# Latent attention: the second rope product of the logits as a 128-row matmul with zero-padded low halves, and narrower raw weight buffers

## The chip, the cores and the metric

The kernel runs on one core of one Trainium2 chip, as one launch. The metric is the device time of that launch in microseconds (us). Engines are named as in the profile: PE is TensorE (PEld its weight loads), DVE is VectorE, ACT is ScalarE, POOL is GpSimd, SP issues the transfers.

## The reference, cut to what matters

The whole program is a stack of layers on 256 tokens of 1024 features, batch 1, all in float32: stick-breaking attention, a gated feed-forward layer with a convolution, forgetting attention, a second feed-forward layer, a pooling layer, and at the end latent attention (MLA) and a final norm. Only latent attention changes. It has 16 heads. A head's query and key have a part of 128 features of its own and a rope part of 64 features; the key's rope part is one for all heads:

```python
q = (rmsnorm_2(q_lat, q_norm_g) @ w_q_b).reshape(B, S, N_HEADS, QK_HEAD_DIM)   # 128 + 64
q_nope, q_rope = q[..., :QK_NOPE_DIM], q[..., QK_NOPE_DIM:]
...
q_rope = apply_rope(q_rope, cos[:, :, None, :], sin[:, :, None, :])
k_rope = apply_rope(k_rope, cos, sin)
...
s = (jnp.einsum('bqhd,bkhd->bhqk', qn, k_nope)
     + jnp.einsum('bqhr,bkr->bhqk', qr, k_rope)).astype(jnp.float32) * scale
s = jnp.where(mask, s, jnp.finfo(jnp.float32).min)
p = jax.nn.softmax(s, axis=-1).astype(v.dtype)
```

## The kernel before, in words

**Numbers in two halves.** Every float32 operand of a matmul is split into a high half and a low half, both of type float32r, and a product is made of three matmuls into one PSUM tile: high by high, high by low, low by high (`mm3`, lines 69 to 72). The high half is a copy on ACT (`hi_copy`, L55), the low half a subtraction on DVE (`lo_sub`, L59). So weights also pass through ACT and DVE before PE can use them.

**Weight streaming.** The weights come in chunks, in the order in which they are used; a chunk comes with one transfer on SP's queue into one of three raw buffers (`RAWB = 3`), each `RAWW` columns of float32 wide. ACT and DVE turn a chunk into parts of at most 1024 columns (tiles `wh`, `wl`, eight buffers each). `bg()` (L182) does this one part at a time and is called at fixed places between PE's work. When the last part of chunk c has been subtracted, `bg_lo` (L173 to L180) asks for chunk c + 3, whose transfer takes the raw buffer that has just come free. So what is counted ahead is chunks, whatever their size.

**Latent attention.** After the latents and their norms (`lat_norm`), `lat_T` (L1092) transposes them: queries' latents to `qT`, keys' to `kT`, and the key's rope part, which stands twice (in rows 0 to 63 and in rows 64 to 127), to `rT`; each with a high and a low tile. The heads are worked on in four groups g of four. For each group there are three chunks or more: two of 256 columns x 8 for the gate z (`m_z`), one of 3 x 768 columns for the queries (`m_q`, 2304 columns in all), one of 2 x 1024 for keys and values (`m_kv`), and in groups 1 to 3 the output projection's rows of the groups before (`m_o`), two chunks a group.

PE's order in the loop over g is written out by hand: `values(g)`, `logits(g, 0)`, `logits(g, 1)` (two heads each), the output projection of group g - 1 or the gate of the next group, `p_T` (transposes of the probabilities), `pv` (probabilities by values), then `q_rope`, `qk` and `rope_T` of the next group. Every engine takes its instructions in program order.

**The logits** (`logits`, L1158) of a pair of heads are made in two blocks: 128 keys for the first 128 queries, then 256 keys for the other 128. In a block each head has three 128-row matmuls for its own features (L70 to L72), then for the rope part one matmul of 128 rows at L1168 and one of 64 rows at L1170. `rope_T` has put a head's high halves in 64 rows of a tile `rq` and its low halves in the other 64 rows, so that the 128-row matmul against `rT`'s high tile does high by high and low by high at once. The 64-row matmul, high by low, reads only the high rows of `rq` and the same rows of `rT`'s low tile. For the pair's first head these are rows 0 to 63, for the second rows 64 to 127.

Of the kernel before, what the change touches and what calls it, by code (L numbers as in the profile page):

```python
# [7 lines left out]
F32 = mybir.dt.float32  # L8
F32R = mybir.dt.float32r
# [6 lines left out]
P = 128  # L16
S = 256
NT = S // P
D = 1024
# [7 lines left out]
RAWW = 2304  # L27
# [8 lines left out]
def tile_net(ctx: ExitStack, tc: tile.TileContext, t, out):  # L36
# [16 lines left out]
    # ---------------------------------------------------------------- helpers  # L53
# [10 lines left out]
    def split(hi, lo, src, scale=None):  # L64
        """src = hi + lo exactly, both of float32r's width"""
        hi_copy(hi, src, 1.0 if scale is None else scale)
        lo_sub(lo, src, hi, scale)
# [6 lines left out]
    def mm3s(ps, ls, rs, first, last):  # L74
        """sum over ls, rs; the low halves of ls last"""
        n = len(ls)
        for m in range(n):
            pe.matmul(ps, lhsT=ls[m][0], rhs=rs[m][0], start=first and m == 0, stop=False)  # L78
            pe.matmul(ps, lhsT=ls[m][0], rhs=rs[m][1], start=False, stop=False)
        for m in range(n):  # L80
            pe.matmul(ps, lhsT=ls[m][1], rhs=rs[m][0], start=False, stop=last and m == n - 1)
# [13 lines left out]
    def at(x, k, c):  # L95
        """columns c of k-tile k, high and low; x a pair of tiles or a list of such pairs,
        each of as many k-tiles"""
# [11 lines left out]
    # ------------------------------------------------------- weight streaming  # L109
    # A chunk [P, a, b] comes in with one transfer and is split in parts of at  # L110
    # most TW columns: by its first dimension ("k") or by columns ("c").  A part
    # is in use until `need` of its columns have gone into TensorE's program.
# [28 lines left out]
    def load_w(upto):  # L141
        while nxt["load"] <= min(upto, len(specs) - 1):
# [3 lines left out]
            # the first ones a part at a time  # L146
# [10 lines left out]
    def bg_hi():  # L157
        """the next part's high half, if there is room for it"""
# [30 lines left out]
    def get_w(i):  # L189
        """function (k, c0, n) -> the split columns of chunk i"""  # L190
# [16 lines left out]
    # ---- the order in which the weights are used  # L207
    def add_v(w, c0):
        """two halves of columns, each in two chunks of four k-tiles"""
# [11 lines left out]
    # the order of the down projection's sum  # L221
# [55 lines left out]
    for g in range(4):  # L277
        add_mz(g)
        wq = t["mla_w_q_b_2"][0][:, 768 * g:768 * (g + 1)]
        W["m_q", g] = rows(wq, 0, 3, need=4 * P + NT * 768)  # L280
# [5 lines left out]
    def get_rows(idx, n=2):  # L286
        """chunks of n k-tiles each -> function (k, c0, n)"""
# [3 lines left out]
    # -------------------------------------------------------------- residual  # L291
# [20 lines left out]
    # ------------------------------------------------------------- constants  # L312
# [7 lines left out]
    # [cos, cos] and [-sin, sin]  # L320
# [3 lines left out]
    # ------------------------------------------------------------------ norms  # L324
    def mean_sq(srcs, n):
        """mean of the squares of the rows of srcs, together n wide, + EPS: summands"""
# [14 lines left out]
    def transpose_split(src, dst, i, b, m=4):  # L341
        """src's column tiles b..b+m -> dst (hi, lo), token tile i"""
# [12 lines left out]
    def scaled(i, r, g):  # L355
        """h's token tile i, by its factor and the gain"""
# [6 lines left out]
    def norm_r(i):  # L363
        """the factor of the norm of h's token tile i"""
# [4 lines left out]
    def square(x, n, ss):  # L369
        """ss = sum of the squares of the rows of x over n"""  # L370
# [4 lines left out]
    # a layer's end: by halves of columns, then the rest  # L375
    def post_add(i, acc, g):
        """h += rmsnorm(acc) * g for token tile i"""
# [28 lines left out]
    # ------------------------------------------------------------ projections  # L406
    def proj_A(ps, aT, w, c0, nk, m=P):
        """ps [m features, S tokens]"""
# [3 lines left out]
    def out_rows(acc, i, oT, w, ks, first, last, by_half=False):  # L412
        """acc [token tile i, D] += o^T rows @ w rows; ks: (k of o^T, k of w)"""
# [8 lines left out]
    def nat_start(aT, views, hook):  # L422
        """two chunks of 256 columns, a token tile at a time; natural in SBUF"""
# [17 lines left out]
    def values_all(xT, views, vv, hooks):  # L441
        """vv = x W, by halves of columns and token tiles; hooks: (half, tile, k) -> what
        comes before the k-th step"""
# [18 lines left out]
    def nat_T(ps, xs, c):  # L462
        """column tile c of nat_start's result, transposed: ps [P, S]"""
# [3 lines left out]
    def edge(tail0, tail1, acc, add, g, dst):  # L467
        """end of a layer: token tile 0 ahead of 1, up to the next layer's
        input; returns that of tile 1, not yet transposed, and the factors"""
# [18 lines left out]
    def attention(s0, s1, s2, s3, post, w_ids, oT, g_post, dst, hook, late, acc0_tile):  # L488
        """the eight pairs of heads, a stage of each a step, in TensorE's
        order; then the output projection up to the next layer's input"""  # L490
# [36 lines left out]
    def heads_out(p, vv, pr, oT):  # L527
        """out^T of the pair's heads into oT"""
# [12 lines left out]
    # per-feature parameters, a feature a partition  # L541
# [22 lines left out]
    # ------------------------------------------------- stick-breaking layer  # L564
# [14 lines left out]
    with tc.tile_pool(name="sb", bufs=2) as sb, tc.tile_pool(name="sbv", bufs=1) as sbv:  # L579
# [6 lines left out]
        # constants of the layer  # L586
# [5 lines left out]
        # -1 where the row (a later key) is at or after the column  # L592
# [22 lines left out]
        def s1(p):  # L615
            qh, ql = st.pop(("qk", p))
            zt = [acc_tile("z") for j in range(2)]
            # z^T, columns (s0: t 0..255, s1: t 128..255), both heads
# [11 lines left out]
            # softplus(z) = max(z, 0) + ln(1 + e^-|z|)  # L630
# [12 lines left out]
        def s2(p):  # L643
            zt, nh, nl, _ = st.pop(("z", p))
            # z - sum of the softplus of the keys from s to t: the logarithm of A
# [35 lines left out]
    # --------------------------------------------------------------- conv FFN  # L681
    # the last steps of the down projection, one token tile after the other
    TAIL = (4, 5)

    def ffn(l, aT, a1, late, dst):
        """a1: token tile 1 of aT, not yet transposed; returns what edge() does;
        late: the gains after and of the next layer's input"""
# [60 lines left out]
    # --------------------------------------------------------- softmax pieces  # L748
    def causal_mask(m):
        """[t of a tile, s of the tile before and the tile itself]"""  # L750
# [4 lines left out]
    def softmax(pl_, zts, cmask, scale, bias=None, bufs=1, ahead=1):  # L755
        """zts: logits of two heads, (t0: 128 keys, t1: 256 keys); the probabilities in SBUF"""
# [29 lines left out]
    def prob_T(pt):  # L786
        """p^T of a head in [s, t] blocks: s0 x (t0, t1), s1 x t1"""
# [5 lines left out]
    with tc.tile_pool(name="fxa", bufs=1) as fxa:  # L793
# [5 lines left out]
        # ------------------------------------------------------ forgetting layer  # L799
        table_set(NLE_SET)  # L800
        with tc.tile_pool(name="fx", bufs=2) as fx, tc.tile_pool(name="fxv", bufs=1) as fxv:
# [17 lines left out]
            # causal mask of a query tile's own keys and those before  # L819
# [5 lines left out]
            # selectors: -1 in row h of each quarter  # L825
# [8 lines left out]
            # forget gates: cumulative log f, [head, t]  # L834
# [70 lines left out]
    # -------------------------------------------------------------- pool layer  # L905
    with tc.tile_pool(name="pl", bufs=2) as pl_, tc.tile_pool(name="plc", bufs=1) as plc:
        # 1 / count of the first 15 positions
# [119 lines left out]
        # MLA's latents: (columns from, columns, weights)  # L1027
# [16 lines left out]
    # --------------------------------------------------------------- MLA layer  # L1044
    with tc.tile_pool(name="ml", bufs=2) as ml, tc.tile_pool(name="mlc", bufs=1) as mlc:
        # the gains of both latents and the mask
# [7 lines left out]
        rT = [mlc.tile([P, 1, S], F32R, name=n) for n in ("rTh", "rTl")]  # L1054

        def rope(dst, src, m, i0, i1, nh):
            """dst, src: [P, token tiles i0..i1, nh, 64]; dst and m, for a product, in SBUF"""
# [34 lines left out]
        def lat_T(i):  # L1092
            transpose_split(lats[i], qT, i, 0, 3)
            transpose_split(lats[i], kT, i, 3, 2)
            transpose_split(lats[i], rT, i, 5, 1)
# [19 lines left out]
        def q_rope(g):  # L1115
            """q's rope part of four heads, natural"""
            wq = st["wq", g] = get_w(W["m_q", g])
# [23 lines left out]
        def rope_T(g):  # L1141
            qr = st.pop(("qr", g))
            pst = mm_tile("pst")
            # of a head: high halves in its own 64 rows, low halves in the others
# [13 lines left out]
        def logits(g, a):  # L1158
            rq = st["rq", g]
            zt = [acc_tile("z") for j in range(2)]  # L1160
            for c0, n, t0 in ((0, P, 0), (P, S, P)):
# [4 lines left out]
                for j in range(2):  # L1166
                    r = slice(64 * j, 64 * j + 64)
                    pe.matmul(zt[j][:, c0:c0 + n], lhsT=rq[j][:, a, t0:t0 + P],  # L1168
                              rhs=rT[0][:, 0, 0:n], start=False, stop=False)
# [272 lines left out]
```

## Time and profile before

| what | value |
|---|---|
| median of 3 runs | 1006.05 us |
| lowest and highest run | 1001.23 and 1006.25 us |
| the profiled execution, span from first to last instruction | 1007.2 us (the page gives no other time for it) |
| PE busy | 992.5 us, 99% of the span |
| DVE, ACT, POOL busy | 754.7, 607.8, 71.6 us |
| mean granted TensorE clock | 0.992 |

A busy PE is not PE at its peak: matmuls overlap, and the profile models their ends. The distance from one matmul's start to the next one's says more than its duration. The clock is given as a share of its upper level: 1.00 is 2.4 GHz, 0.50 is 1.2 GHz. Latent attention takes the last 200 us or so of the span.

### The profile page before, as it was taken

Reading aid. Unit: us, or ns where it says so; the run is one execution under the profiler, and the core shown is the slowest. Engines: PE = TensorE matmul, PEld = TensorE weight load, DVE = VectorE, ACT = ScalarE, POOL = GpSimd, SP = SyncE. Lnnn points to the kernel's source line nnn. Section 1 sums busy time; section 2 is a strip of 40 time slices with the busy share of each in tenths; the row PEclk is TensorE's granted clock in tenths of the full one; section 3 lists DMA queues with packets and bytes.
Section 4 is the critical chain, followed back from the end, with each engine's and each line's share of the span. In section 5 each row is a group of like instructions: output and inputs, shape, how many; then the busy total and the mean of one; then the engine's idle time right before and its main releaser. Section 6 shows DMA issues by size and latency. Waiting matters only on the chain.

```text
span 1007.2 us, 17578 instructions
## 1 busy us (share of the span) xinstructions
PE 992.5 (99%) x6955; PEld 909.0 (90%) x6955; DVE 754.7 (75%) x1297; ACT 607.8 (60%) x1050; POOL 71.6 (7%) x180
## 2 busy tenths in 40 slices
PE   8999999999999999999999999999999999999997
PEld 6899789999887899889999988999998899888986
DVE  5577788899745879877999944777677766967675
ACT  5489867677534657566667633664543546746563
POOL 1022220000002000020000000200000110110100
PEclk8999999999999999999999999999999999999999
DMA  8823346575752744426565664466554453534411
GB/s 292 258 86 145 126 163 214 167 244 177 251 183 79 239 134 168 142 84 209 185 224 179 202 240 143 153 224 230 170 167 146 145 186 123 172 127 138 159 66 42
DMA packets 116228, 170.79 MB, mean 170 GB/s; under 512 B 4162, under 2 KB 93618, under 8 KB 116146
## 3 DMA queue, kind: packets, MB, share of 16 engines
q1 hardware_dynamic: 116082, 169.68, 50.6%
q8 instruction: 54, 0.88, 0.4%
q14 instruction: 28, 0.23, 0.1%
q0 software_dynamic: 64, 0.00, 0.0%
HBM read 168.62 MB, written 1.05 MB: 168 GB/s over the span
## 4 chain that ended last, share of the span: by engine, by line
PE 93%; DVE 2%; ACT 2%; POOL 1%; DMA 1%; issue 1%; SPq 0%; POOLq 0%; DVEq 0%; ACTq 0%
PE psu L70 10%; PE psu L72 10%; PE psu L71 10%; PE accD L71 4%; PE accD L72 4%; PE accD L70 4%; PE psq L70 4%; PE psq L72 4%; PE psq L71 4%; PE accO L70 3%; PE accO L72 3%; PE accO L71 3%; PE accP L72 1%; PE accP L70 1%; PE accP L71 1%; PE accV L78 1%
## 5 line engine op out<-in xcount | busy, mean ns | idle before, releaser
L59 DVE TENSOR_TENSOR wl<-raw,wh 128x1024 fp32r<-128x1024 f32 (+3 forms) x300 | 353.0, 1197 | 105.9 <-ACT wh L55 103.1
L55 ACT ACTIVATE wh<-raw 128x1024 fp32r<-128x1024 f32 (+3 forms) x316 | 315.3, 1026 | 99.1 <-PE accD L72 44.2
L70 PE MATMUL psu<-aT,wh 128*128 128x256 f32 x864 | 241.7, 280 | 0.0
L72 PE MATMUL psu<-aT,wl 128*128 128x256 f32 x864 | 240.9, 279 | 0.0
L71 PE MATMUL psu<-aT,wh 128*128 128x256 f32 x864 | 240.8, 279 | 0.0
L72 PEld LDWEIGHTS psu<-aT,wl 128*128 128x128 f32 x864 | 162.3, 188 | 0.0
L70 PEld LDWEIGHTS psu<-aT,wh 128*128 128x128 f32 x864 | 162.1, 188 | 0.2
L71 PEld LDWEIGHTS psu<-aT,wh 128*128 128x128 f32 x864 | 162.0, 187 | 0.0
L703 DVE SCALAR_TENSOR_TENSOR yc<-psu,conv,yc 128x255 f32<-128x255 f32 (+1 forms) x160 | 73.4, 479 | 7.6 <-ACT yc L696 4.6
L70 PE MATMUL accD<-wh,gh 128*128 128x512 f32 x176 | 69.3, 394 | 0.0
L71 PE MATMUL accD<-wl,gh 128*128 128x512 f32 x176 | 69.3, 394 | 0.0
L72 PE MATMUL accD<-wh,gl 128*128 128x512 f32 x176 | 69.3, 394 | 0.0
L335 POOL TENSOR_TENSOR ss<-ss,epsc 128x1 f32<-128x1 f32 x24 | 10.9, 453 | 628.2 <-ACT junk L372 628.1
L70 PE MATMUL psq<-aT,wh 128*128 128x256 f32 x192 | 54.1, 282 | 0.1
L71 PE MATMUL psq<-aT,wh 128*128 128x256 f32 x192 | 53.5, 279 | 0.0
L72 PE MATMUL psq<-aT,wl 128*128 128x256 f32 x192 | 53.5, 278 | 0.0
L708 ACT ACTIVATE yc<-yc 128x256 f32<-128x256 f32 x44 | 18.4, 418 | 55.0 <-DVE yc L703 55.0
L696 ACT ACTIVATE yc<-psu,conv 128x256 f32<-128x256 f32 x80 | 40.3, 554 | 7.6 <-PE psu L72 7.6
L71 PEld LDWEIGHTS accD<-wl,gh 128*128 128x128 f32 x176 | 32.9, 187 | 8.1
L72 PEld LDWEIGHTS accD<-wh,gl 128*128 128x128 f32 x176 | 32.9, 187 | 8.1
L70 PEld LDWEIGHTS accD<-wh,gh 128*128 128x128 f32 x176 | 32.9, 187 | 8.1
L55 ACT ACTIVATE qkh<-psq 128x512 fp32r<-128x512 f32 x32 | 19.0, 594 | 33.0 <-PE psq L72 32.8
(331 smaller groups left out, 2288.9 us busy)
## 6 DMA issues: line engine op xcount, KB each, us to landing
raw<-in_w_up_dram SPq DMA_DIRECT2D x44, 1024.0 KB, 5.1
raw<-in_w_down_dram SPq DMA_DIRECT2D x22, 1024.0 KB, 5.0
raw<-in_pool_w_in_dram SPq DMA_DIRECT2D x16, 1024.0 KB, 7.1
raw<-in_sb_w_qkv_dram SPq DMA_DIRECT2D x10, 1024.0 KB, 6.1
raw<-in_w_kvf_dram SPq DMA_DIRECT2D x8, 1024.0 KB, 5.7
raw<-in_pool_w_out_dram SPq DMA_DIRECT2D x8, 1024.0 KB, 5.9
raw<-in_mla_w_in_dram SPq DMA_DIRECT2D x8, 1024.0 KB, 5.4
raw<-in_mla_w_out_dram SPq DMA_DIRECT2D x8, 1024.0 KB, 5.5
```

Source lines behind the costliest of these rows:

```text
L55: act.activation(out=hi, in_=src, func=AF.Copy, scale=scale)
L59: (eng or dve).tensor_tensor(out=lo, in0=src, in1=hi.bitcast(F32), op=ALU.subtract)
L70: pe.matmul(ps, lhsT=l[0], rhs=r[0], start=first, stop=False)
L71: pe.matmul(ps, lhsT=l[0], rhs=r[1], start=False, stop=False)
L72: pe.matmul(ps, lhsT=l[1], rhs=r[0], start=False, stop=last)
L78: pe.matmul(ps, lhsT=ls[m][0], rhs=rs[m][0], start=first and m == 0, stop=False)
L335: pool.tensor_tensor(out=s0, in0=s0, in1=epsc[:, 0:1], op=ALU.add)
L696: act.activation(out=y[:, u, :], in_=ps[:, u * S:(u + 1) * S], func=AF.Identity, bias=cp[:, 132 + q:133 + q], scale=cp[:, 88 + q:89 + q])
L703: dve.scalar_tensor_tensor(out=y[:, u, d:S], in0=ps[:, u * S:(u + 1) * S - d], scalar=w, in1=y[:, u, d:S], op0=ALU.mult, op1=ALU.add)
L708: act.activation(out=y[:, 0, :], in_=y[:, 0, :], func=AF.Gelu_apprx_tanh)
```

## The change

The key's rope part gets one high tile as before (`rTh`) and two low tiles, one for each head of a pair. `rTl[0]` has the low halves in rows 0 to 63 and zeros in rows 64 to 127, `rTl[1]` the other way round. The zeros are written once by POOL. The second rope matmul takes all 128 rows of `rq` and of the head's own low tile; the rows of low halves in `rq` meet zeros. `lat_T` does the rope part by itself, with one DVE subtraction for each of the two low tiles. The raw buffers shrink from 2304 to 2048 columns, which the query chunk does not fit; it becomes two chunks of 2 x 768 and 1 x 768 columns, read through `get_rows` instead of `get_w`. The parts and their order stay the same. The rest of the diff takes comments and docstrings out and moves line numbers.

```diff
-RAWW = 2304
+RAWW = 2048
...
-        W["m_q", g] = rows(wq, 0, 3, need=4 * P + NT * 768)
+        W["m_q", g] = [rows(wq, 2 * c, 2 - c, need=4 * P + NT * 768) for c in range(2)]
...
-        rT = [mlc.tile([P, 1, S], F32R, name=n) for n in ("rTh", "rTl")]
+        rTh = mlc.tile([P, S], F32R, name="rTh")
+        rTl = [mlc.tile([P, S], F32R, name=f"rTl{j}") for j in range(2)]
+        for j in range(2):
+            pool.memset(rTl[j].bitcast(F32), 0.0)
...
-            transpose_split(lats[i], rT, i, 5, 1)
+            ps = mm_tile("psT")
+            pe.transpose(ps[:, 0:P], lats[i][:, tok(5)], ident)
+            hi_copy(rTh[:, tok(i)], ps[:, 0:P])
+            for j in range(2):
+                r = slice(64 * j, 64 * j + 64)
+                lo_sub(rTl[j][r, tok(i)], ps[r, 0:P], rTh[r, tok(i)])
...
-            wq = st["wq", g] = get_w(W["m_q", g])
+            wq = st["wq", g] = get_rows(W["m_q", g])
...
                 for j in range(2):
-                    r = slice(64 * j, 64 * j + 64)
-                    pe.matmul(zt[j][:, c0:c0 + n], lhsT=rq[j][:, a, t0:t0 + P],
-                              rhs=rT[0][:, 0, 0:n], start=False, stop=False)
-                    pe.matmul(zt[j][:, c0:c0 + n], lhsT=rq[j][r, a, t0:t0 + P],
-                              rhs=rT[1][r, 0, 0:n], start=False, stop=True)
+                    for x in (rTh, rTl[j]):
+                        pe.matmul(zt[j][:, c0:c0 + n], lhsT=rq[j][:, a, t0:t0 + P], rhs=x[:, 0:n],
+                                  start=False, stop=x is not rTh)
```

On PE, the four rope matmuls of one block of the logits (first pair of heads, 128 keys; `rq` with its number is one head's tile):

```order
-L1168 MATMUL z<-rTh,rq_9525 128x128
-L1170 MATMUL z<-rTl,rq_9525 128x128
-L1168 MATMUL z<-rTh,rq_9526 128x128
-L1170 MATMUL z<-rTl,rq_9526 128x128
+L1178 MATMUL z<-rTh,rq_9532 128x128
+L1178 MATMUL z<-rTl_9078,rq_9532 128x128
+L1178 MATMUL z<-rTh,rq_9533 128x128
+L1178 MATMUL z<-rTl_9079,rq_9533 128x128
```

Their number and place stay; the second and the fourth now read a low tile of their own, over all rows.

On SP's queue, the weight transfers of latent attention from the first query chunk to the second group's (`mla_w_in` is the gate z, `mla_w_q_b` the queries, `mla_w_kv_b` keys and values, `mla_w_out` the output projection):

```order
-L153 DMA raw<-in_mla_w_q_b_dram 128x3x768
+L153 DMA raw<-in_mla_w_q_b_dram 128x2x768
+L153 DMA raw<-in_mla_w_q_b_dram 128x768
 L153 DMA raw<-in_mla_w_kv_b_dram 128x2x1024
 L153 DMA raw<-in_mla_w_in_dram 128x8x256 x2
-L153 DMA raw<-in_mla_w_q_b_dram 128x3x768
+L153 DMA raw<-in_mla_w_q_b_dram 128x2x768
+L153 DMA raw<-in_mla_w_q_b_dram 128x768
 L153 DMA raw<-in_mla_w_kv_b_dram 128x2x1024
 L153 DMA raw<-in_mla_w_out_dram 128x2x1024 x2
```

The order of the data is the same, but each query chunk takes two places. With three buffers, `m_kv` now waits for the buffer of the second chunk of z instead of the first, and the first chunk of `m_o` for the buffer of the query chunk's first piece instead of z's second chunk.

On DVE, the end of `lat_T` for one tile of 128 tokens (`psT` is the transposed latent, `wl` a weight part's low half):

```order
 L59 TENSOR_TENSOR kTl<-psT,kTh 128x2x128
-L59 TENSOR_TENSOR rTl<-psT,rTh 128x128
+L59 TENSOR_TENSOR rTl_9078<-psT,rTh 64x128
+L59 TENSOR_TENSOR rTl_9079<-psT,rTh 64x128
 L59 TENSOR_TENSOR wl<-raw,wh 128x768
```

One subtraction over 128 rows becomes two over 64 rows, ahead of the query weights' first part.

## Rows read from the trace of the kernel before

**Rows 1.** The page's head and its part 1, PE (busy us, share, instructions).
```profile
span 1007.2 us, 17578 instructions
PE 992.5 (99%) x6955; PEld 909.0 (90%) x6955; DVE 754.7 (75%) x1297; ACT 607.8 (60%) x1050; POOL 71.6 (7%) x180
```

**Rows 2.** The page's part 4, shares of the chain that ended last.
```profile
PE 93%; DVE 2%; ACT 2%; POOL 1%; DMA 1%; issue 1%; SPq 0%; POOLq 0%; DVEq 0%; ACTq 0%
```

**Rows 3.** Timeline of PE, first logits of group 0: start, duration (us), instruction, count.
```profile
837.85 0.27 PE L1168 MATMUL z<-rTh,rq 128*128 128x128 f32 x1
838.05 0.32 PE L1170 MATMUL z<-rTl,rq 64*128 64x128 f32 x1
...
838.81 0.39 PE L70 MATMUL z<-qkh 128*128 128x256 f32 x1
839.04 0.28 PE L71 MATMUL z<-qkl,qkh 128*128 128x256 f32 x1
...
839.64 0.28 PE L1168 MATMUL z<-rTh,rq 128*128 128x256 f32 x1
839.85 0.38 PE L1170 MATMUL z<-rTl,rq 64*128 64x256 f32 x1
...
840.78 0.33 PE L70 MATMUL z<-qkh 128*128 128x128 f32 x1
840.95 0.27 PE L71 MATMUL z<-qkl,qkh 128*128 128x128 f32 x1
```

**Rows 4.** Timeline of PE, logits of the forgetting layer, all of 64 rows.
```profile
361.56 0.28 PE L878 MATMUL z<-qkh,qkl 64*128 64x256 f32 x2
361.68 0.28 PE L883 MATMUL z<-F,sel 64*128 64x256 f32 x2
361.88 0.38 PE L70 MATMUL psq<-fTh,wh 128*128 128x256 f32 x1
```

**Rows 5.** Timelines of DVE and PE, first probabilities of group 0.
```profile
849.31 1.02 DVE L59 TENSOR_TENSOR pl<-pT,ph 128x384 fp32r<-128x384 f32 x2
...
853.48 0.28 PE L70 MATMUL po<-ph,vh 128*128 128x256 f32 x1
```

**Rows 6.** Timelines of SP, DVE and ACT, the weights behind group 0's logits.
```profile
848.10 11.53 SPq L153 DMA_DIRECT2D raw<-in_mla_w_out_dram  x2
...
857.41 4.10 DVE L59 TENSOR_TENSOR wl<-raw,wh 128x768 fp32r<-128x768 f32 x4
...
862.53 1.05 ACT L55 ACTIVATE wh<-raw 128x1024 fp32r<-128x1024 f32 x1
...
863.61 1.29 DVE L59 TENSOR_TENSOR wl<-raw,wh 128x1024 fp32r<-128x1024 f32 x1 [1.44 <-ACT wh L55]
```

**Rows 7.** DMA issues from 780 us on: count, KB each, us to landing.
```profile
raw<-in_mla_w_out_dram SPq DMA_DIRECT2D x8, 1024.0 KB, 5.5
```

**Rows 8.** Timeline of PE, the first values matmul of group 1.
```profile
869.34 0.50 PE L70 MATMUL psv<-wh,kTh 128*128 128x512 f32 x1 [0.17 <-DVE qkl L59]
```

**Rows 9.** Timelines of SP and DVE around the first query and key weights.
```profile
817.24 5.06 SPq L153 DMA_DIRECT2D raw<-in_mla_w_in_dram  x2
...
817.93 0.28 DVE L59 TENSOR_TENSOR rTl<-psT,rTh 128x128 fp32r<-128x128 f32 x1
...
824.97 3.45 DVE L59 TENSOR_TENSOR wl<-raw,wh 128x1024 fp32r<-128x1024 f32 x2
```

**Rows 10.** Timeline of PE, second logits up to the transposes, groups 1 and 2.
```profile
878.28 0.36 PE L70 MATMUL z<-qkh 128*128 128x256 f32 x1
...
888.45 0.82 PE L790 MATMUL pT<-ident,pt 128*128 128x128 f32 x6
...
926.98 0.28 PE L70 MATMUL z<-qkh 128*128 128x256 f32 x1
...
934.18 0.82 PE L790 MATMUL pT<-ident,pt 128*128 128x128 f32 x6
```

**Rows 11.** Windows; last columns are granted clock, DMA share, GB/s.
```profile
880.00:882.00 2.00, 2.00 (x5) 1.36 (x6) 1.97 (x9) 0.75 (x4) 0.00 (x0) 0.50 0.35 88
```

## The prediction

> **What bounds the kernel now.** I read the page first: PE is busy for 99% of a span of 1007.2 us [rows 1], and PE makes up 93% of the chain that ended last, while DVE, ACT and POOL have 2%, 2% and 1% of it [rows 2]. So a microsecond that PE gains is a microsecond gained, as long as no other engine is late at the place. Busy time doesn't tell whether PE is at its pace, so I read the timeline of PE in the logits next, from start to start [rows 3]. Among the matmuls of 128 rows a step is 0.12 us: five of them from 839.04 to 839.64. From the first rope matmul on the steps grow: 837.85 to 838.05 is 0.20, and the four rope matmuls with the matmul behind them take 837.85 to 839.04. The same rows with 256 keys show 839.64 to 840.95. The reader is to see that the long steps begin and end with the matmuls of 64 rows, and that the matmul after the last of them is slow too.
>
> Is a matmul of 64 rows slow by itself, or the change between 64 and 128 rows? In the forgetting layer's logits all have 64 rows [rows 4]. There a pair takes one step of 0.12 us, 361.56 to 361.68, so 0.06 each; the step from the last pair to the first 128-row matmul is 0.20. So the change of height costs, not the half height.
>
> **The rope matmuls, 32 of them in 16 blocks.** Their number stays. The block of 128 keys has five steps from the first rope matmul to the second one behind the block: 839.04 - 837.85 = 1.19 us. Five ordinary steps are 0.60, which saves 0.59. The block of 256 keys has 840.95 - 839.64 = 1.31, which saves 0.71. A call of `logits` has both, 1.30 us; eight calls give 10.4 us. The bounds: nothing saved if something other than the height sets these steps; and if the steps came down to the 0.06 of the forgetting layer's pairs, five would be 0.30, a call would save 1.90 and the eight 15.2. That end is out of reach, since those pairs work in different rows, and a padded matmul has no rows left for a neighbour. I take 10.4, because all matmuls in these blocks then have the form of those that make the 0.12 steps.
>
> Here a rule speaks against the change. The trace of the rope blocks shows no 64-row matmul beside another one [rows 3]. The Trainium skill, TensorE: Matmul & The Clock Gate (Part 3, packing small matmuls), says that matmuls of few rows run at the same time when they stand in different row groups, so that padding them to 128 rows would give a gain away. By that rule the 32 padded matmuls would lose 0.06 each, 1.9 us; by the row nothing is lost, since a 128-row matmul stands between any two of them. It is a rival below.
>
> **Does the gain reach the end?** In group 0 the two calls bring PE 2.6 us forward, while DVE, which works without a pause there, is not faster. PE's first product of probabilities and values at 853.48 would come at 850.88; DVE is through with the probabilities' low halves at 849.31 + 1.02 = 850.33 [rows 5]. That leaves 0.5 us, the tightest place. In groups 1 to 3 the output projection stands between, and there is more room. So DVE nearly becomes the bound, but doesn't.
>
> **The weights, which come later by one chunk.** The query chunk becomes two, so with three buffers each transfer behind it waits for a buffer one chunk younger. The first chunk of `m_o` started at 848.10, with great reserve. Now it waits until DVE has subtracted the query chunk's second part. That is the first of four parts that begin at 857.41 and take 4.10 us together [rows 6]; by columns it has 768 of 3584, 0.88 us, and ends at 858.3. A transfer of this size lands 5.5 us later [rows 7], at 863.8. ACT began to convert it at 862.53, DVE stood idle for 1.44 us until that was done [rows 6]. So conversion begins 1.3 us late. Behind it on ACT and DVE stand the rope products of the next queries and the splits of the next queries and keys, and for one of these PE already waits 0.17 us to get a PSUM buffer at 869.34 [rows 8]. All of the 1.3 us therefore reaches PE. If the whole stretch moves 2.6 us forward, so does each of these times. Bounds: 0, if the reserve of DVE is larger than these rows let see, and 5.5, a whole landing. I take 1.3, once.
>
> The first `m_kv` chunk gets the place in time of the transfer that started at 817.24 [rows 9]. It lands at 822.7 and takes ACT two conversions of 1.05 us each [rows 6], until 824.8; DVE takes it up at 824.97 [rows 9]. ACT's wait is covered by 0.2 us; without that cover each further microsecond of landing costs one. In groups 1 to 3 there are two chunks of `m_o` and two of the gate between, and the loads are due long after they land. Four more transfers on SP, which mostly waits, cost nothing.
>
> **DVE and POOL.** Two more subtractions of 0.28 us [rows 9], before the query weights' first part: 0 to 0.56, depending on whether PE waits for these parts. I take 0.3. The two clearings on POOL come when the tile's former users are long done; POOL's mean instruction is 71.6/180 = 0.4 us [rows 1], so 0.8 at most, and with 1% of the chain I take 0.
>
> **The clock.** In the second logits of group 1 the granted clock is at its lower level, 1.2 GHz (0.50) [rows 11]. From 878.28 to 888.45 the stretch takes 10.17 us, the same instructions in group 2 take 7.20, from 926.98 to 934.18 [rows 10]: 3.0 us. What PE did before: it waited for DVE [rows 8] and then went through the slow steps of the logits. The change removes the slow steps and lengthens the wait by 1.3 us. Groups 0, 2 and 3 have the slow steps too, but not the waits, and no fall of the clock. So the fall may go or stay. The three runs lie at 1006.05, 1001.23 and 1006.25; one without the fall would be 3.0 lower, which fits the lowest in sign, though not in all its size. I take it as gone, at little better than even odds.
>
> **The sum.** -10.4 + 1.3 + 0.3 = -8.8 us at an unchanged clock. The profiled execution goes from 1007.2 to 998.4; the median of the runs is 1.15 below its span, so 997.2. Without the fall of the clock, 994.2, which I round to 994.
>
> **The rivals.**
> - The fall of the clock stays: 997.2. For it: the longer wait ahead of the place. Against: the denser logits.
> - DVE or ACT becomes the bound in the loop: for it, DVE is at work without a pause from the logits to the probabilities, and the reserve in group 0 is 0.5 us. If each group gives back half of its 2.6 us, the gain shrinks by 5.2 and the time is 1002.4 with the fall of the clock and 999.4 without.
> - The change doesn't do what it says: the steps stay as they are, and the weights still come late: 1006.05 + 1.6 = 1007.7. If padding also lost the 0.06 us a matmul that the pairs of [rows 4] gain by running in different rows, 1.9 more: 1009.6. (That is the Trainium skill's rule of row groups, named above.) Against both, the 0.20 at the change of height in [rows 4] and the lone 64-row matmuls in [rows 3].
> - Slower: the late loads hit every group. The first `m_o` chunk shows the mechanism. Were each group to wait for a whole landing and one conversion, 5.5 + 1.05, the four lose 26 us against 10.4 gained: about 1022. It decides from 2.6 us a group on. Against it: only group 0 calls for its weights so closely behind each other.
> - More than forecast: the wait for `m_o` is absorbed, and the start too is like that of the lowest run: 1001.23 - 10.1, about 991.
>
> **How the numbers follow.** Forecast 50%, clock stays 30%, DVE bound 10%, no gain 4%, slower 3%, more 3%. Some 0.5% is what a measurement of this kernel can tell from no change, 5 us, so the border of faster is 1001.0. Forecast, staying clock, the last case and half of the DVE case lie beyond it: 0.88. The other half of the DVE case and the case of no gain make 0.09 for no difference, the late loads 0.03. The range reaches from 990, just under the last case, to 1000.5, which takes in the staying clock with 3 us to spare and half of the DVE case.
>
> **What would show it.** In the profile after, the steps among the rope matmuls should be 0.11 to 0.12, and a call of `logits` 1.3 us shorter. The first `m_o` transfer should start some 10 us later relative to the probabilities of group 0, ACT should wait for it, and PE should wait 1 us or more for DVE at the first values of group 1. The clock at the second logits of group 1 tells the first two cases apart. I am wrong if the steps stay above 0.2, or if PE waits for DVE or ACT ahead of the products of probabilities and values, or for the weights in groups 1 to 3.

## The result, and the profile after

| what | before | changed | ratio (95% interval) |
|---|---|---|---|
| median of 4 runs each, us | 1006.15 | 994.76 | 0.9892 (0.9865 to 0.992) |
| lowest and highest run, us | 1001.23, 1007.92 | 993.05, 996.7 | |
| the profiled execution: span, mean clock | 1007.2, 0.992 | 992.6, 0.997 | |

The forecast was 994.0, between 990 and 1000.5. The changed kernel is faster by 1.1%. Its page's head and part 1, and its shares of the chain that ended last, answer to [rows 1, 2]:

```profile
span 992.6 us, 17595 instructions
PE 977.5 (98%) x6955; PEld 900.3 (91%) x6955; DVE 754.3 (76%) x1299; ACT 608.4 (61%) x1050; POOL 72.4 (7%) x182
...
PE 92%; DVE 3%; ACT 2%; DMA 1%; issue 1%; POOL 1%; SPq 0%; POOLq 0%; DVEq 0%; ACTq 0%
```

PE has the same 6955 matmuls and 15 us less busy time; DVE has two instructions more, the split subtractions, and POOL two, the clearings. Busy time can't tell whether this came from shorter steps or from a faster clock, so the timeline of PE comes next: first logits of group 0, changed kernel (start, duration in us, instruction, count):

```profile
835.54 0.27 PE L1178 MATMUL z<-rTh,rq 128*128 128x128 f32 x1
835.65 0.28 PE L1178 MATMUL z<-rTl,rq 128*128 128x128 f32 x1
...
835.99 0.33 PE L70 MATMUL z<-qkh 128*128 128x256 f32 x1
836.16 0.28 PE L71 MATMUL z<-qkl,qkh 128*128 128x256 f32 x1
...
836.75 0.28 PE L1178 MATMUL z<-rTh,rq 128*128 128x256 f32 x1
836.87 0.28 PE L1178 MATMUL z<-rTl,rq 128*128 128x256 f32 x1
...
837.23 0.22 PE L70 MATMUL z<-qkh 128*128 128x128 f32 x1
837.29 0.28 PE L71 MATMUL z<-qkl,qkh 128*128 128x128 f32 x1
```

From the first rope matmul to the second matmul behind the block, 835.54 to 836.16 is 0.62 us where it was 1.19, and 836.75 to 837.29 is 0.54 where it was 1.31 [rows 3]. The two calls of a group, from the first logits matmul to the first matmul behind them, take 4.61 us, 834.93 to 839.54; they took 7.20, 837.23 to 844.43 (lines below). Four groups give 10.36.

Two stretches ahead of the logits became longer. Their first and last matmul, and with `psz` the first matmul behind the two calls of group 0, before:

```profile
814.21 0.82 PE L345 MATMUL psT<-ident,lat 128*128 128x128 f32 x6
...
837.23 0.22 PE L70 MATMUL z<-qkh 128*128 128x128 f32 x1
...
844.43 0.39 PE L70 MATMUL psz<-aT,wh 128*128 128x256 f32 x1
...
861.77 0.28 PE L70 MATMUL psq<-qTh,wh 128*128 128x256 f32 x1
...
872.58 0.22 PE L70 MATMUL z<-qkh 128*128 128x128 f32 x1
```

and in the changed kernel:

```profile
811.20 0.71 PE L345 MATMUL psT<-ident,lat 128*128 128x128 f32 x5
...
834.93 0.22 PE L70 MATMUL z<-qkh 128*128 128x128 f32 x1
...
839.54 0.28 PE L70 MATMUL psz<-aT,wh 128*128 128x256 f32 x1
...
856.87 0.28 PE L70 MATMUL psq<-qTh,wh 128*128 128x256 f32 x1
...
868.40 0.22 PE L70 MATMUL z<-qkh 128*128 128x128 f32 x1
```

The **latent stretch**, from `lat_T` to group 0's logits, goes from 23.02 to 23.73 us, +0.71. The **group 1 stretch**, from its first query product to its logits, goes from 10.81 to 11.53, +0.72. What PE waits for in them is in the view of waits for 800 to 993 us, changed kernel (total, times, longest; `psr` is the PSUM tile of the queries' rope part, `psq` that of a head's queries and keys, `psv` that of the values):

```profile
PE psv L70 <- DVE qkl L59: 0.6, 1, 0.6
PE psq L72 <- DVE wl L59: 0.5, 1, 0.5
PE psr L71 <- DVE wl L59: 0.3, 1, 0.3
```

Before, the same view had only 0.2 and 0.3 us in the first two of these lines and no third. The weights behind group 0, as they come now (changed kernel, timelines of SP, DVE, ACT and PE):

```profile
853.51 1.24 SPq L153 DMA_DIRECT2D raw<-in_mla_w_out_dram  x2
...
852.52 4.10 DVE L59 TENSOR_TENSOR wl<-raw,wh 128x768 fp32r<-128x768 f32 x4
...
858.41 1.06 ACT L55 ACTIVATE wh<-raw 128x1024 fp32r<-128x1024 f32 x1 [0.67 <-DMA raw<-in_mla_w_out_dram]
...
862.51 1.06 ACT L55 ACTIVATE wh<-raw 128x1024 fp32r<-128x1024 f32 x1 [1.12 <-DMA raw<-in_mla_w_out_dram]
...
859.50 1.22 DVE L59 TENSOR_TENSOR wl<-raw,wh 128x1024 fp32r<-128x1024 f32 x1 [2.22 <-ACT wh L55]
...
865.17 0.50 PE L70 MATMUL psv<-wh,kTh 128*128 128x512 f32 x1 [0.59 <-DVE qkl L59]
```

The reader is to see the chain against [rows 6, 8]: SP asks for `m_o` one query part after DVE began with them, ACT waits for both chunks, DVE's idle time grows from 1.44 to 2.22, PE's wait at `psv` from 0.17 to 0.59. A part of the loss stands ahead of that wait, where the view names none: from 861.86 to 862.33, between the second head's products and the third's, two steps of PE take 0.47 us, where two ordinary ones take 0.23.

Against [rows 5], the probabilities of group 0 and the first product that needs them (changed kernel, timelines of DVE and PE):

```profile
846.88 1.02 DVE L59 TENSOR_TENSOR pl<-pT,ph 128x384 fp32r<-128x384 f32 x2
...
848.58 0.28 PE L70 MATMUL po<-ph,vh 128*128 128x256 f32 x1
```

The last view is the clock at the second logits of group 1, where before had 0.50 [rows 11]:

```profile
880.00:882.00 2.00, 2.00 (x10) 1.63 (x9) 2.00 (x4) 1.71 (x4) 0.00 (x0) 1.00 0.00 0
```

It stays at its upper level. **The account of the two profiled spans:** -10.36 + 0.71 + 0.72 = -8.93 for the change, -3.0 for the clock in group 1 (10.17 against 7.20 us by [rows 10]), and -3.01 because this execution reached `lat_T` sooner (811.20 against 814.21), where the two programs are still alike. That makes -14.9 against the -14.6 measured. The other 0.3 is not assigned; this execution took 43.59 us from group 1's first logits to group 2's (868.40 to 911.99), a second one of the same kernel, below, 43.05.

### The profile page after: what moved, and what is told of

It reads as the page before. It is cut to its first block, busy times and chain, and to the rows that moved or that the text cites. A ratio compares the mean times of both kernels' runs of the same rounds, so it can differ in the third digit from the quotient of the medians.

```text
span 992.6 us, 17595 instructions
## 1 busy us (share of the span) xinstructions
PE 977.5 (98%) x6955; PEld 900.3 (91%) x6955; DVE 754.3 (76%) x1299; ACT 608.4 (61%) x1050; POOL 72.4 (7%) x182
## 4 chain that ended last, share of the span: by engine, by line
PE 92%; DVE 3%; ACT 2%; DMA 1%; issue 1%; POOL 1%; SPq 0%; POOLq 0%; DVEq 0%; ACTq 0%
PE psu L70 10%; PE psu L71 10%; PE psu L72 10%; PE accD L71 4%; PE accD L72 4%; PE accD L70 4%; PE psq L70 4%; PE psq L72 4%; PE psq L71 4%; PE accO L70 3%; PE accO L72 3%; PE accO L71 2%; PE accP L71 2%; PE accP L72 2%; PE accP L70 2%; PE psT L345 1%
```

## The experiments

The theory: mixing 64-row and 128-row matmuls costs the steps, all of the gain comes from there, and the two losses come from the late `m_o` chunks and from the extra subtractions. The rivals: the weights' new order brings some of the gain; padding as such is needed; the clock makes the difference.

**The parts by themselves.** One kernel has the padded matmul without the narrower buffers (one low tile stands in a buffer of the gains, for room), one has the narrower buffers and the two query chunks alone. Against the changed kernel, the first is

```diff
-RAWW = 2048
+RAWW = 2304
...
-        W["m_q", g] = [rows(wq, 2 * c, 2 - c, need=4 * P + NT * 768) for c in range(2)]
+        W["m_q", g] = rows(wq, 0, 3, need=4 * P + NT * 768)
...
-        rTl = [mlc.tile([P, S], F32R, name=f"rTl{j}") for j in range(2)]
+        rTl = [mlc.tile([P, S], F32R, name="rTl0"),
+               gp.tile([P, D], F32, tag="g", name="rTl1")[:, 0:S].bitcast(F32R)]
...
-            wq = st["wq", g] = get_rows(W["m_q", g])
+            wq = st["wq", g] = get_w(W["m_q", g])
```

> The matmul part alone: padded low tiles (the second one in a buffer of the gains, since it does not fit elsewhere), but the query weights in one chunk and raw buffers of 2304 columns as before. If the height of the matmuls sets the long steps, all rope matmuls step by 0.11 to 0.12 us, a call of logits is 1.3 us shorter, and the time is that of the changed kernel less the late weights' 0.7 us: about 994, with ACT not waiting for the output projection's weights behind group 0's logits and PE waiting at most 0.4 us for DVE at the values of group 1. If a good part of the gain came from the loads or from the narrower buffers, it stays above 998.

and the second is the edits of the buffers and of the query chunk the other way round, made in the kernel before.

> The loads alone: query weights in two chunks and raw buffers of 2048 columns, the rope matmuls as before. If the late weights only cost, the time is that of the kernel before or up to 1.3 us more (1006 to 1007.5), ACT waits 0.7 to 1.3 us for the first weights of the output projection, and the clock falls in group 1 as before, or elsewhere. If the loads are part of the gain, it is below 1003.

Measured: 994.65 us for the matmul alone, ratio 0.9883 (0.9858 to 0.9907); 1007.4 for the loads alone, 1.0014 (0.9998 to 1.003). The stretches say more than the totals: with the matmul alone the calls of a group take 4.62 us, the latent stretch 23.73, the group 1 stretch 10.81. With the loads alone the latent stretch is 23.00 and the group 1 stretch 11.52. So the gain and the 0.71 at the latents belong to the matmul's part, the 0.72 in group 1 to the loads. The waits of ACT in the kernel with the loads alone are those of the changed kernel:

```profile
861.83 1.06 ACT L55 ACTIVATE wh<-raw 128x1024 fp32r<-128x1024 f32 x1 [0.66 <-DMA raw<-in_mla_w_out_dram]
...
865.76 1.06 ACT L55 ACTIVATE wh<-raw 128x1024 fp32r<-128x1024 f32 x1 [0.95 <-DMA raw<-in_mla_w_out_dram]
```

**Is it the padding, or the mixing?** Two kernels keep the 64-row matmuls of before. One puts the two of a block next to each other:

```diff
                 for j in range(2):
-                    r = slice(64 * j, 64 * j + 64)
                     pe.matmul(zt[j][:, c0:c0 + n], lhsT=rq[j][:, a, t0:t0 + P],
                               rhs=rT[0][:, 0, 0:n], start=False, stop=False)
+                for j in range(2):
+                    r = slice(64 * j, 64 * j + 64)
                     pe.matmul(zt[j][:, c0:c0 + n], lhsT=rq[j][r, a, t0:t0 + P],
                               rhs=rT[1][r, 0, 0:n], start=False, stop=True)
```

> As before the change, without padding, but in each block of the logits the two 128-row rope matmuls first and then the two 64-row ones, next to each other in different rows. If a change of height costs and not the half height: two changes a block instead of four, the second 64-row matmul starts 0.06 us after the first, a block loses some 0.35 us of its 0.6 to 0.7 us excess, a call 0.7, the kernel 5 to 6: about 1000. If a 64-row matmul is slow by itself (its weights can not be loaded ahead), the steps stay at 0.25 to 0.31 and the time at 1006.

The other puts all four of a call at its end:

```diff
-                        (qh[:, S:S + n], ql[:, S:S + n]), True, False)
+                        (qh[:, S:S + n], ql[:, S:S + n]), c0 == 0, False)
+                for j in range(2):
+                    pe.matmul(zt[j][:, c0:c0 + n], lhsT=rq[j][:, a, t0:t0 + P],
+                              rhs=rT[0][:, 0, 0:n], start=False, stop=False)
+            for c0, n, t0 in ((0, P, 0), (P, S, P)):
                 for j in range(2):
                     r = slice(64 * j, 64 * j + 64)
-                    pe.matmul(zt[j][:, c0:c0 + n], lhsT=rq[j][:, a, t0:t0 + P],
-                              rhs=rT[0][:, 0, 0:n], start=False, stop=False)
                     pe.matmul(zt[j][:, c0:c0 + n], lhsT=rq[j][r, a, t0:t0 + P],
-                              rhs=rT[1][r, 0, 0:n], start=False, stop=True)
+                              rhs=rT[1][r, 0, 0:n], start=False, stop=c0 > 0)
```

> As before the change, without padding, but the four 64-row matmuls of a call of logits gathered at its end: two changes of height a call instead of eight. If only changes cost: excess of a call 0.3 us instead of 1.3, less 0.24 for the 64-row pairs side by side, so a call within 0.2 us of the padded one, and, with no late weights, a time of 994 to 996. If the half height costs by itself: no gain, 1006. If the softmax behind is delayed by the later end of the first block, PE waits ahead of the transposes of the probabilities and the gain is smaller.

Measured: 997.4 us, ratio 0.9916 (0.9893 to 0.9938), for the pairs, and 993.96, ratio 0.9874 (0.9852 to 0.9897), for the four gathered. A group's calls take 5.40 and 4.81 us, against 7.20 before and 4.61 padded. PE with the pairs, first block:

```profile
836.01 0.38 PE L1167 MATMUL z<-rTh,rq 128*128 128x128 f32 x2
836.33 0.33 PE L1171 MATMUL z<-rTl,rq 64*128 64x128 f32 x2
836.59 0.39 PE L70 MATMUL z<-qkh 128*128 128x256 f32 x1
836.81 0.28 PE L71 MATMUL z<-qkl,qkh 128*128 128x256 f32 x1
```

and with four gathered:

```profile
835.41 0.40 PE L1167 MATMUL z<-rTh,rq 128*128 128x256 f32 x2
835.74 0.50 PE L1172 MATMUL z<-rTl,rq 64*128 64x128 f32 x4
836.16 0.33 PE L70 MATMUL z<-qkh 128*128 128x128 f32 x1
```

The second row holds four matmuls, two of 128 and two of 256 keys. They take 0.42 us with the step out of them. The two 128-row matmuls ahead take 0.33 instead of 0.24, two steps of 0.12: the step into the 64-row matmuls is longer too. So the loss goes with the number of changes of height: four in a block before, two a block with the pairs, two a call when gathered, none when padded. Against a padded call, a call loses 1.30 us with eight changes, 0.40 with four and 0.10 with two. That is not in proportion, because the two of a pair start less than 0.01 us apart (0.06 was expected), take one step in place of two and so give 0.12 back, 0.24 a call. With that counted, a change costs 0.16, 0.16 and 0.17 us; this is an estimate from the four times of a group's calls and the step of 0.12. A padded matmul takes a full step; what it saves is the change. The pairs gained more than was expected of them, 1.80 us a group or 7.2 in all, where 5 to 6 stood in the expectation. The Trainium skill's rule (TensorE: Matmul & The Clock Gate, Part 3), that matmuls of few rows in different row groups run at the same time, agrees: a pair takes 0.33 us, where one by itself took 0.32 [rows 3]. What a change of height costs does not follow from that rule, and it decides in this kernel.

**The late weights.** The query chunk cut into 1 x 768 and 2 x 768 columns instead of 2 and 1:

```diff
-        W["m_q", g] = [rows(wq, 2 * c, 2 - c, need=4 * P + NT * 768) for c in range(2)]
+        W["m_q", g] = [rows(wq, c, 1 + c, need=4 * P + NT * 768) for c in range(2)]
...
-            wq = st["wq", g] = get_rows(W["m_q", g])
+            wqs = [get_w(x) for x in W["m_q", g]]
+            wq = st["wq", g] = lambda k, c0, m: wqs[k > 0](k - (k > 0), c0, m)
```

> The changed kernel, but the query weights' two chunks are 1 x 768 and 2 x 768 columns instead of 2 x 768 and 1 x 768, so that the output projection's first weights wait for a buffer that comes free one part, some 7 us, earlier. If the late weights come from the place of the chunk border, ACT no longer waits for the output projection's weights in group 0, the stretch from group 1's first q matmul to its first logits goes back from 11.5 to 10.8 us, and the time is 0.7 us below the changed kernel's (not to be told from it by the time alone). If DMA bandwidth is what makes them late, the stretch stays at 11.5.

> The cut into 1 x 768 and 2 x 768 columns alone, once more beside the next kernels on one chip: 993.3 us as before, ratio 0.986, lat_T stretch 23.7 us, group 1's stretch from the first query transposition to the logits 10.8.

The changed kernel itself ran beside the first of these:

> The changed kernel once more, beside the other two on one chip: 994 to 996, mean clock 0.995 or more, the stretch from group 1's first q matmul to its first logits 11.5 us.

Measured: 993.29 us, ratio 0.9859 (0.9841 to 0.9877), and again 992.06, 0.9865 (0.9832 to 0.9897). The changed kernel beside it: 995.49, 0.9881 (0.9865 to 0.9898). The group 1 stretch is 10.81 us in the first, 10.80 in the second, and 11.42 in the repeat of the changed kernel. In the first of them, the transfer of `m_o` stands at 851.49 and its conversion waits for nothing:

```profile
851.49 5.96 SPq L153 DMA_DIRECT2D raw<-in_mla_w_out_dram  x2
...
854.34 3.47 ACT L55 ACTIVATE wh<-raw 128x768 fp32r<-128x768 f32 x4
860.34 1.04 ACT L55 ACTIVATE wh<-raw 128x1024 fp32r<-128x1024 f32 x1
```

The first query piece is one part, so its buffer is free one part sooner: 8.85 us lie between the transfer and the conversion, where the changed kernel has 4.90 and waits. Against group 0's first product of probabilities and values the transfer starts 4.7 us earlier than in the changed kernel, not the 7 expected. The late weights are thereby shown as the cause of the 0.72. From group 0's first logits to the end of the span both executions take 156.4 us, the repeat of the changed kernel 157.0, so the gain is kept as far as the end. The intervals of the totals overlap; the stretch is what settles it. The second median of this version, 992.06, is the lowest of all that ran; its first, 993.29, and the intervals don't set it apart from the other padded kernels.

**The subtractions.** The same cut, and in `lat_T` one DVE subtraction over all rows again, whose halves POOL copies into the two padded tiles:

```diff
+            lo_sub(rTt[:, tok(i)], ps[:, 0:P], rTh[:, tok(i)])
             for j in range(2):
                 r = slice(64 * j, 64 * j + 64)
-                lo_sub(rTl[j][r, tok(i)], ps[r, 0:P], rTh[r, tok(i)])
+                pool.tensor_copy(rTl[j][r, tok(i)], rTt[r, tok(i)])
```

> The changed kernel with the query chunk cut into 1 x 768 and 2 x 768 columns, and with one DVE subtraction a token tile over all 128 rows in lat_T as before; POOL then copies the two halves into the two zero-padded tiles. If the two extra DVE subtractions are what delays PE in lat_T, the stretch from the first latent transpose to group 0's first logits goes from 23.7 back to 23.0 us, PE's 0.25 us wait for the query weights' low half at 819.82 shrinks, and the time is 0.7 below that of the 1 + 2 cut alone (ratio 0.9852 to before where that has 0.9859). If the delay comes from splitting the tile rTl as such, or from the weights behind it, the stretch stays at 23.7. Slower by up to 1 us if POOL's four copies come late for the first logits, 15 us behind.

Measured: 992.2 us, ratio 0.9867 (0.9837 to 0.9898). The latent stretch is back at 23.01 us, and PE's wait of 0.25 at `psr` is gone. DVE in the changed kernel:

```profile
814.91 0.58 DVE L59 TENSOR_TENSOR rTl<-psT,rTh 64x128 fp32r<-64x128 f32 x2
815.53 0.96 DVE L59 TENSOR_TENSOR wl<-raw,wh 128x768 fp32r<-128x768 f32 x1
...
817.33 0.58 DVE L59 TENSOR_TENSOR rTl<-psT,rTh 64x128 fp32r<-64x128 f32 x2
817.94 1.83 DVE L59 TENSOR_TENSOR wl<-raw,wh 128x768 fp32r<-128x768 f32 x2
```

and in this one:

```profile
817.91 0.28 DVE L59 TENSOR_TENSOR rTt<-psT,rTh 128x128 fp32r<-128x128 f32 x1
818.11 0.95 DVE L59 TENSOR_TENSOR wl<-raw,wh 128x768 fp32r<-128x768 f32 x1
...
819.77 0.28 DVE L59 TENSOR_TENSOR rTt<-psT,rTh 128x128 fp32r<-128x128 f32 x1
820.07 1.92 DVE L59 TENSOR_TENSOR wl<-raw,wh 128x768 fp32r<-128x768 f32 x2
```

From the rope subtraction to the query part behind it DVE takes 0.62 and 0.61 us in the changed kernel, 0.20 and 0.30 here: 0.42 and 0.31, together 0.73, which is what PE loses. So the extra subtractions are the cause. They cost more than their length, because the split also ends an overlap: in `lat_T` of the kernel before and here, a DVE instruction over all rows mostly starts 0.08 us before the one ahead of it ends, while in the changed kernel the subtraction in rows 64 to 127 and the query part behind it start 0.01 and 0.03 us after that end. Whether the change of the starting row does this was not varied by itself; the two 64-row subtractions of `rq` (`rope_T`), alike in both kernels, start 0.03 us behind as well. In the median the 0.7 us doesn't show against the cut alone (992.2 and 992.06), but the profiles have it: from the first latent transpose to the end of the span this one takes 179.4 us, the cut alone 180.1 in both its profiles, and from group 0's first logits on all three take 156.4. The 0.7 is kept as far as the end. The medians also hold the unlike start, of which more below.

**The clock.** Both kernels have the matmul part of the change alone (one query chunk). In one, only group 1 keeps the 64-row matmuls; in the other, only group 1 is padded:

```diff
-                        pe.matmul(zt[j][:, c0:c0 + n], lhsT=rq[j][:, a, t0:t0 + P], rhs=x[:, 0:n],
+                        r = slice(64 * j, 64 * j + 64) if g == 1 and x is not rTh else slice(0, P)
+                        pe.matmul(zt[j][:, c0:c0 + n], lhsT=rq[j][r, a, t0:t0 + P], rhs=x[r, 0:n],
```

> The matmul part alone (one query chunk, raw buffers of 2304 columns), but in group 1 the second rope matmul has 64 rows as before the change. If the fall of the clock in group 1 needs the slow steps of that group's own logits, it falls there in most runs as in the kernel before, with a mean clock of 0.994 or less in most runs and a time of 994.6 + 2.6 + 2 to 3 = 999 to 1000. If it hangs on when the program gets there (the start, or what lies ahead), the clock stays at 0.995 or more and the time is 994.6 + 2.6 = 997.2.

> Only group 1's second rope matmuls are padded (one query chunk as before); groups 0, 2 and 3 keep the 64-row ones. The steps alone: 2.6 us of 10.4 saved, +0.7 for the subtractions. If it is the slow steps of group 1 that let the clock fall, the fall is gone in nearly all runs (mean clock 0.995 or more) and the time is 1006.2 - 2.6 + 0.7 - 2.5 = 1001.8 us. If any group's slow steps can bring it on, it comes in another group instead, the mean clock stays at 0.990 to 0.994 in most runs, and the time is 1004.3.

(The second has `g != 1`.) Measured: 996.92 us, ratio 0.9898 (0.988 to 0.9916), and 1001.78, 0.9977 (0.995 to 1.0003). The first kernel's profiled execution has the fall, again in group 1 (windows; the columns are those of [rows 11]):

```profile
870.00:874.00 4.00, 4.00 (x23) 3.10 (x22) 3.90 (x14) 3.97 (x7) 0.00 (x0) 1.00 0.23 28
874.00:878.00 4.00, 4.00 (x14) 2.92 (x14) 3.93 (x12) 3.08 (x8) 0.00 (x0) 0.62 0.69 270
878.00:882.00 4.00, 4.00 (x11) 3.09 (x11) 3.86 (x16) 2.81 (x9) 0.00 (x0) 0.52 0.79 259
```

From 800 us on PE waits twice in this profile, at 821.34 and 827.69, more than 40 us ahead of the fall. Three of the twelve profiles have such a fall, each 5.7 to 5.8 us behind the first logits matmul of group 1, which has the mixed order in all three: before (878.33), the loads alone (877.60) and this one (874.99).

But this kernel's other five runs have a mean clock of 0.996 or more, and the median is near the 997.2 of the second outcome named. So slow steps in one group seldom bring the clock down; that the place in the program decides instead, as that outcome had it, isn't shown. With only group 1 padded, five of twelve runs lie at 0.988 to 0.994 and seven at 0.995 or more. That lies between the two outcomes; the median has the 1001.8 of the first because it falls among the seven. By these means group 1's steps are not the only ones that can bring the clock down.

A mean clock counts the start and the end of the program too. The profiled run of the pairs has 0.994, and yet no fall in between (a window, columns as above):

```profile
16.00:990.00 974.00, 968.78 (x6911) 891.14 (x6909) 746.32 (x1285) 598.50 (x1031) 68.53 (x165) 1.00 0.51 170
```

None of the nine profiles without a fall is below 0.994, the three with one are at 0.991 and 0.992. So 0.994 alone doesn't show a fall, and the count takes 0.993 or less. That stands in 26 of 45 runs of before, in 8 of 12 with the loads alone, in 4 of 12 with only group 1 padded, in one of six with only group 1 unpadded, in none of six with the pairs, and in none of the 36 runs of kernels in which no group has the mixed order (the padded ones, the changed one, the gathered one), where the lowest is 0.995. The gathered kernel has no zeros, so it isn't the zeros that keep the clock up. Where in the other groups it falls, no profile here shows.

## Why the prediction was right, step by step

- **The rope matmuls: right.** Predicted 10.4 us by steps of 0.12 from the neighbouring matmuls, measured 10.36. The pairs and the gathered four show the mechanism named, the change of height. The rival in which padding loses 0.06 a matmul is excluded as a loss against before; against the gathered four a padded call is 0.10 shorter, not longer (half of 4.81 - 4.61).
- **The gain reaches the end: right.** From group 0's first logits to its first product of probabilities and values were 16.25 us (837.23 to 853.48), and are 13.65 now, 834.93 to 848.58: all of the 2.60. DVE's probabilities end 0.68 us ahead of it (846.88 + 1.02 against 848.58), 0.5 were forecast. The view of waits has none of PE in groups 2 and 3. So the rival in which DVE becomes the bound is excluded.
- **The late weights: mechanism right, term mis-sized.** 1.3 us forecast, 0.72 measured. The transfer starts where the prediction put it, one query part after DVE's first, and 10.3 us later than before against the first product of probabilities and values, where some 10 were forecast. The step that failed is "lands 5.5 us later": ACT had the chunk 4.90 after the issue and waited 0.67. The second chunk, which the prediction didn't reckon, made ACT wait longer, 1.12. Conversion began 9.83 us behind that product, 9.05 before [rows 5, 6]: 0.78 late, and of that 0.72 reached PE, so "all of it reaches PE" nearly held. That PE would wait 1 us or more at `psv` was too much: 0.59.
- **The extra subtractions: mis-sized beyond the bound.** 0.3 forecast with 0.56 as the upper end, 0.71 measured. The bound came from the duration of one subtraction, 0.28, twice. What counts is the time from start to start on DVE: two subtractions of 64 rows took 0.62 and 0.61 where one of 128 rows took 0.20 and 0.30. The term left out the overlap with the neighbours, which the split ends.
- **The `m_kv` load: right.** ACT waits 1.68 us for it now, but with the subtractions mended the latent stretch is 23.01 with that wait still there, so it is covered.
- **The clock: right as the forecast had it**, at little better than even odds. That the time came within 1 us of 994.0 is in part luck: the fall is worth 3 us either way, and the two mis-sized terms (0.6 too much, 0.4 too little) nearly cancel, -8.93 against -8.8. Of the two things that the prediction saw ahead of the fall, the wait and the slow steps, the wait isn't needed: the fall with group 1 unpadded came without one. At a mean clock of 0.995 or more, eight runs of before have a median of 1003.75, nine of the changed kernel 995.02: 8.7 us, which is about the change without the clock (the runs come from several chips). The medians of all 45 and all nine, 1006.89 and 995.02, are 11.9 apart; the other 3.1 are the size of one fall of the clock, 3.0. That the slow steps are needed for the fall is borne out by the counts, as no kernel without them shows it; they are not enough, since in the profiles of before, of the loads alone and of only group 1 padded other groups have them and no fall. Why it came in group 1 and not in others is open.

## What to carry to other kernels

Here matmuls of 64 rows among full ones cost by the number of changes, so pad such matmuls where rows are unused, or gather them; here both gave 2.4 to 2.6 us of 7.2. By the estimate above, the two changes around a row of pairs cost some 0.33 us together and each pair gives 0.12 back, so gathering would overtake padding from three pairs in a row on; no run here has three. When a chunk is cut in two, the prefetch counted in chunks shrinks: look at which part frees the buffer, and cut so that the first piece is the small one. Bound a short instruction by the distance between starts of its neighbours, not by its duration, and expect a split by rows to cost more than one instruction's length.

## What the runs showed of the hardware

- A step at a change between 64 and 128 rows took 0.20 to 0.31 us; by the estimate above a change costs 0.16. Two 64-row matmuls next to each other, in rows 0 to 63 and 64 to 127, took one step. With full height the 40 matmuls of a group's two padded calls took 4.61 us, 0.115 each, at the upper level of the clock.
- The clock falls in the middle of a program while PE is busy throughout: in before's profile from 878.3 us for 6.8 us, in the kernel with group 1 unpadded from 875.0 for the same 6.8. The slower steps ahead of it are all that the rows show of a cause, and other groups have them without a fall.
- The start, alike in all kernels, is not alike in time: the first latent transpose comes between 809.74 and 814.21 us in the twelve profiles. At 8 to 16 us the mean clock is 0.58 in before and 0.79 in the changed kernel, but the repeat of the changed kernel has 1.00 there and arrives at 812.98, so the clock at the start is not the whole of it. The kernels with all groups padded lie at 810.22 to 814.20, the four with none at 810.80 to 814.21: the 3.01 us in the account of the two spans are not the change's.
- Of two transfers of 1 MB issued behind each other the second took longer: the second `m_o` chunk was ready about 8 us after its issue (854.75 at the latest, to 862.51), the first after 4.90.
- A DVE subtraction in rows 64 to 127 behind one in rows 0 to 63 started 0.01 us after the other's end (815.20, changed kernel), and the instruction over all rows behind it 0.03 us after; over all rows in sequence, the next one started 0.08 us before the end (817.93 and 818.13, before).
